# Fourier position steps: sums and differences of mirrored blocks written once, the first gate product reading them at exchanged places

## The chip, the cores and the metric

The kernel runs on one core of one Trainium2 chip. The metric is the device time of one execution in microseconds (us). Three executions took 1563.1, 1563.9 and 1565.81 us; the median is 1563.9 us.

## What is computed

The reference is a two-layer encoder trunk on two sequences, 2048 and 512 positions of 1024 channels, in fp32. Layer 0 is windowed attention. Layer 1, where the change lies, mixes by a Fourier transform in four groups of 256 channels:

```
h = rmsnorm(x, g)
hg = h.reshape(b, s, 4, 256)
f = fftn(hg, axes=(1, 3), norm="ortho").real.reshape(b, s, d)
x = x + (f * silu(h @ w_gate)) @ w_out
```

A final rmsnorm follows. The input is real, so the transform over a group's channels has a mirrored half: with A and B the two products of the position transform with the cosine and the sine columns, the real part at channel c is A - B or A + B, at the mirrored channel the other of the two; and the row of positions that mirrors a row has the two signs exchanged.

## The kernel before

**The order of the work.** First the attention runs, chunk by chunk. Then a Fourier phase (`fourier_phase`) runs through pairs of 128-position tiles: norm, transposes, channel transform (`z_odd_even`) and gate projection (`gates`). The results are combined over tiles by radix steps. From about 1296 us on come the *position steps*: each takes one residue k1 of the positions, multiplies it by cosine and sine tables (tile ABp in PSUM), multiplies by the gate and transposes the result (tile tw); `finish` then multiplies it with the output weights (tile fo) and adds the residual x. The steps run in the order s1, s0, s2 (the short sequence), p0 and p8, p4, p2, p6, and then p1, p7, p3, p5.

**Two blocks in a step.** p0, p8, s0 and s2 write one block of 128 output rows. The eight other steps write two: the row k1 and its mirror 16 - k1 (or 4 - k1). They take both from the same products A and B. The mirror's rows come out turned around, which the later transposes undo.

**What `position` (lines 1672 to 1714) does.** It works in two halves (`hf`) of two groups each. For each half it splits the operands (`halves_of`, line 1664, tile gp: a high part cast by the scalar engine and a low part subtracted by the vector engine), and three matmuls for each operand use them: high by high, high by low, low by high. Then, in each group of 256 columns, the columns 0 to 128 hold A (line 1701, copied by the scalar engine into the first block's tile up_0) and the sums and differences of A and B go as follows:

- up_1, columns 0 and 128: A, four elements copied by the scalar engine (line 1704)
- up_1, columns 1 to 127: A + B (line 1705); columns 129 to 255: A - B (line 1706)
- up_0, columns 129 to 255: A + B (line 1707); columns 1 to 127: A - B, in place (line 1708)

So a step with two blocks has four vector instructions of 128 x 254 elements per half, and one with a single block two (1707 and 1708). At the end the vector engine multiplies each tile of 1024 columns by its gate tile s2p (line 1711; 1713 for step s1, which hands the products to a list that runs later, after line 1473). The mirror's gate rows come by a gather on GpSimd's queue (line 1648), the other's by a load on SP's queue (line 1645).

**What sets the order.** Between s1 and p6 a scheduler orders each engine's instructions by priorities and by its own estimate of when operands are there, so that an edit of `position` moves the neighbours. From step p1 on, much of the vector engine's order is tied by hand (`seq`, `after`, `chain`). PSUM tiles, SBUF tiles of the pools "L", "R", "hT" and "x", and the queues of SP and GpSimd are taken in program order.

Of the kernel before, what the change touches and what calls it, by code (L numbers as in the profile page):

```python
# [14 lines left out]
ALU = mybir.AluOpType  # L15
# [5 lines left out]
P = 128  # L21
# [34 lines left out]
def encoder(  # L56
# [3 lines left out]
    PE, ACT, DVE, POOL, SP = nc.tensor, nc.scalar, nc.vector, nc.gpsimd, nc.sync  # L60
# [35 lines left out]
    def bank(name):  # L96
        if turning:
            return two_banks(name)[:, 0]
        return banks[-1].tile([P, 512], F32, tag="bank", name=name)
# [3 lines left out]
    def two_banks(name):  # L103
        return turning[0].tile([P, 2, 512], F32, tag="two", name=name)
# [29 lines left out]
    def matmul3(out, a, b, start, stop, more=False, behind=None):  # L134

        for i, j in ((0, 0), (0, 1), (1, 0)):
            ins = pe(PE.matmul(out, a[i], b[j], start=start and i + j == 0, stop=stop and i == 1, skip_group_check=more))  # L137
            after(ins, behind)
        return ins
# [53 lines left out]
    def after(ins, anchor):  # L193

        if anchor is not None:
            tc.add_manual_dep(ins.ins, anchor.ins.name, ISSUE, reason="issue order")
# [1022 lines left out]
    def fourier_phase(tail):  # L1219
        with ExitStack() as es:  # L1220
# [14 lines left out]
            def zt(name):  # L1235
                return right([P, D], F32, name)
# [167 lines left out]
            last_z, last_c, last_mix = [None], [None], [None] * 3  # L1404
# [246 lines left out]
            def position_loads(name, tab, tiles):  # L1651
                return [gated(name, r, xtile) for r in tiles], table(name, tab, left)

            def halves_of(name, gr, gs, hf, after_one=None):

                out = []
                for i, g in enumerate((gr, gs)):
                    if i and after_one:
                        after_one()
                    if g is not None:  # L1660
                        t = main.tile([P, 2, 512], F32R, align_bytes=LINE, tag="hT", bufs=8, name=f"g{name}_{hf}_{i}")
                        gv = g[hf] if isinstance(g, list) else g[:, hf * 512 : hf * 512 + 512]
                        ACT.copy(t[:, 0], gv)
                        low = DVE.tensor_tensor(t[:, 1], gv, f32(t[:, 0]), ALU.subtract)
                        if chain.get("steps"):
                            seq("dve", low)
                        out.append(t)
                return out

            last_b, last_read, gated_by = [None], [None], []  # L1670

            def position(name, tab, gr, gs, tiles, loads=None, parts=None, between=None, later=None):

                s2s, tb = loads or position_loads(name, tab, tiles)
                cs, sn, ns = [(tb[:, 2 * i], tb[:, 2 * i + 1]) for i in range(3)]
                bp = None if turning else bank(f"B{name}")
                us = [zt(f"u{name}_{i}") for i in range(len(tiles))]
                for hf in range(2):
                    if hf and between:
                        between()  # L1680
                    ts = parts[hf] if parts and parts[hf] else halves_of(name, gr, gs, hf)

                    def acc(out, tabs, c0, n):
                        for i, (w, t) in enumerate(zip(tabs, ts)):
                            v = [
                                t[:, part].rearrange("p (g c) -> p g c", g=2)[:, :, c0 : c0 + n]
                                for part in range(2)
                            ]
                            end = matmul3(out, w, v, i == 0, i == len(ts) - 1)
                        return end  # L1690

                    if turning:
                        ab = two_banks(f"AB{name}_{hf}")
                        a, b = ab[:, 0, :260], ab[:, 1, :256]
                    else:
                        a, b = bank(f"A{name}_{hf}")[:, :260], bp[:, hf * 256 : hf * 256 + 256]
                    a, b = (t.rearrange("p (g c) -> p g c", g=2) for t in (a, b))
                    chain["A"] = acc(a, (cs, ns), 0, 130)
                    chain["B"] = acc(b, (sn, cs), P, P)
                    uv = [u.rearrange("p (g c) -> p g c", g=4)[:, 2 * hf : 2 * hf + 2] for u in us]  # L1700
                    ACT.copy(uv[0][:, :, 0 : P + 1], a[:, :, 0 : P + 1])
                    re, im = uv[0][:, :, 1:P], b[:, :, 1:P]
                    for v in uv[1:]:
                        ACT.copy(v[:, :, 0 : P + 1 : P], a[:, :, 0 : P + 1 : P])
                        DVE.tensor_tensor(v[:, :, 1:P], re, im, ALU.add)
                        DVE.tensor_tensor(v[:, :, P + 1 : 256], re, im, ALU.subtract)
                    DVE.tensor_tensor(uv[0][:, :, P + 1 : 256], re, im, ALU.add)
                    last_b[0] = DVE.tensor_tensor(re, re, im, ALU.subtract)
                for u, s2 in zip(us, s2s):
                    if later is None:  # L1710
                        gated_by.append(DVE.tensor_tensor(u, u, s2, ALU.mult))
                    else:
                        later.append(lambda u=u, s2=s2: after(DVE.tensor_tensor(u, u, s2, ALU.mult), last_c[0]))
                return list(zip(us, tiles))

            def out_rows(r):
# [222 lines left out]
            def step(*positions):  # L1939
                new = [t for p in positions for t in position(*p)]  # L1940
                if pend:
                    end = finish(*pend.pop(0))
                if turning:
                    chain["turns"] = end
                    new = turned(new)
                else:
                    new = [(split_T(u, f"u{r[0]}", r[2] is not None), r) for u, r in new]
                for f in pend:
                    finish(*f)
                pend[:] = new  # L1950
# [48 lines left out]
            def sums_behind():  # L1999
# [10 lines left out]
                1: [lambda: f_load(1), lambda: early.append(sample(0, (0,), (left,), (xtile,), left, True))],  # L2010
                2: [lambda: f_load(2), lambda: early.append(sample(2, (1,), (left,), (xtile,), left, True))],
                3: [lambda: first.extend(position(*one, later=products)), lambda: f_load(3)],
                4: [lambda: [f() for f in products], lambda: f_load(4)],
                5: [lambda: turn_first(0), sums_behind],
                6: [lambda: turn_first(1)],
            })
            new = position(*early[0])
            f_split(4)
            new += position(*early[1])
# [12 lines left out]
            for i, l in enumerate((w0, w2)):  # L2032
                for a in range(3):
                    t = zt(f"ev{a}_{i}")
# [33 lines left out]
            for a in range(4):  # L2068
                for i, l in enumerate((pc, qs)):
# [3 lines left out]
                    t = zt(f"od{a}_{i}")  # L2073
# [205 lines left out]
```

## Time and profile before

| | |
|---|---|
| median of three executions | 1563.9 us |
| the profiled execution | 1564.1 us, its span 1562.3 us |
| tensor engine (PE) busy | 1545.1 us |
| vector engine (DVE) busy | 1148.0 us |
| scalar engine (ACT) busy | 889.3 us |
| GpSimd (POOL) busy | 454.5 us |
| mean granted clock of PE | 0.999 |

The span runs from the first to the last instruction; the time of an execution contains a little more. Times in the trace count from the span's start. A row of a timeline gives the start, the duration, the engine, the line of the code, the operation, the written tile, the tiles that are read, the shape and count; in brackets stands how long the engine sat idle before it and what ended that. PEld is the weight load of the tensor engine, which overlaps its matmuls. SPq and POOLq are the queues from which transfers are issued.

### The profile page before, as it was taken

To read this page: it belongs to the slowest core of one execution; us is meant where nothing else is said; L and a number is where in the kernel's file an instruction comes from. 1 tells how busy PE (TensorE), PEld (TensorE's weight loads), DVE (VectorE), ACT (ScalarE), POOL (GpSimd) and SP (SyncE) were. 2 spreads that over 40 slices of the span, in tenths; PEclk is the share of its full clock that TensorE was granted. 3 is DMA by queue.
4 is the path that set the end of the run, shared out by engine and by line. 5 is a ranking of instruction groups with operands and counts; after the bars stand their busy time and mean duration, and the time that the engine had idled before them with its cause. 6 is when DMAs were issued, how large, how long until landed. Compare 5 with 4: busy or idle time off the path is not lost.

```text
span 1562.3 us, 33420 instructions
## 1 busy us (share of the span) xinstructions
PE 1545.1 (99%) x12958; PEld 1355.5 (87%) x12958; DVE 1148.0 (73%) x2503; ACT 889.3 (57%) x1956; POOL 454.5 (29%) x616
## 2 busy tenths in 40 slices
PE   9999999999999999999999999999999999999998
PEld 7899888999898888988888899988888888888886
DVE  5888655777537776367764577768989888989896
ACT  6788534787237784257861477736656564333353
POOL 2565652421414313314214242223122211101100
PEclk9999999999999999999999999999999999999999
DMA  9677687685856765866639666665575669556852
GB/s 330 230 274 240 224 336 271 217 291 167 314 198 223 241 232 195 311 212 201 257 132 363 232 204 228 247 249 199 206 242 188 222 233 400 197 202 255 298 189 94
DMA packets 100730, 372.70 MB, mean 239 GB/s; under 512 B 11235, under 2 KB 22251, under 8 KB 83420
## 3 DMA queue, kind: packets, MB, share of 16 engines
q1 hardware_dynamic: 82716, 297.38, 55.3%
q0 software_dynamic: 16688, 70.04, 11.4%
q10 hardware_dynamic: 1168, 3.15, 0.6%
q8 instruction: 102, 1.67, 0.4%
q14 instruction: 56, 0.46, 0.1%
HBM read 280.06 MB, written 90.47 MB: 237 GB/s over the span
## 4 chain that ended last, share of the span: by engine, by line
PE 89%; DVE 6%; DMA 2%; ACT 1%; issue 1%; POOL 0%; POOLq 0%; ACTq 0%; DVEq 0%; SPq 0%
PE pj L527 27%; PE av L753 7%; PE W L137 6%; PE pj L137 6%; PE tp L137 5%; PE av L137 5%; PE spt L653 5%; PE spt L137 4%; PE tp L712 4%; PE Wo L137 3%; PE Z L137 3%; PE fo L137 3%; PE z L1392 2%; PE Zo L137 2%; PE X L137 1%; PE ABp L137 1%
## 5 line engine op out<-in xcount | busy, mean ns | idle before, releaser
L527 PE MATMUL pj<-h,wg 64*128 64x512 f32 x1920 | 438.9, 389 | 0.0
L527 PE MATMUL pj<-h,wq 64*128 64x512 f32 x1560 | 379.2, 389 | 1.2 <-DVE qab L571 1.2
L527 PEld LDWEIGHTS pj<-h,wg 64*128 64x128 f32 x1920 | 330.6, 184 | 23.1
L527 PEld LDWEIGHTS pj<-h,wq 64*128 64x128 f32 x1560 | 284.5, 184 | 22.0 <-DVE qab L571 2.7
L672 DVE CUSTOM_DVE_ANT_0 S<-spt,b 128x385 f32<-128x385 f32 (+1 forms) x320 | 165.1, 525 | 92.3 <-PE spt L653 88.3
L680 ACT ACTIVATE S<-S 128x385 f32<-128x385 f32 (+1 forms) x320 | 189.1, 592 | 63.2 <-DVE S L672 41.6
L725 ACT CAST pts<-tp 128x768 fp32r<-128x768 f32 (+1 forms) x160 | 121.2, 758 | 95.4 <-PE av L753 60.0
L729 DVE TENSOR_TENSOR pts<-tp,pts 128x768 fp32r<-128x768 f32 (+1 forms) x160 | 144.1, 901 | 13.5 <-ACT pts L725 12.8
L753 PE MATMUL av<-pts,v 64*128 64x256 f32 x1680 | 143.5, 287 | 3.0 <-DVE pts L729 3.0
L753 PEld LDWEIGHTS av<-pts,v 64*128 64x128 f32 x1680 | 127.2, 186 | 7.3 <-DVE pts L729 3.8
L798 POOL TENSOR_TENSOR uT<-o,uT 128x256 fp32r<-128x256 f32 x75 | 56.7, 756 | 244.1 <-ACT uT L794 243.9
L653 PE MATMUL spt<-kwin,qab 64*128 64x384 f32 (+1 forms) x960 | 121.0, 338 | 0.9 <-DVE S L672 0.7
L137 PE MATMUL fo<-wo,tTu 128*128 128x512 f32 x480 | 115.1, 392 | 0.0
L137 PEld LDWEIGHTS fo<-wo,tTu 128*128 128x128 f32 x480 | 88.4, 188 | 17.3
L712 PEld LDWEIGHTS tp<-ident,S 64*128 64x128 f32 x1792 | 93.2, 137 | 10.2 <-DVE pts L729 3.1
L712 PE MATMUL tp<-ident,S 64*128 64x64 f32 x1792 | 97.9, 224 | 0.1
L789 POOL TENSOR_TENSOR o<-o,s 128x256 f32<-128x256 f32 x75 | 55.7, 742 | 120.7 <-DVE o L783 95.3
L695 DVE TENSOR_SCALAR S<-S 128x384 f32<-128x384 f32 (+1 forms) x192 | 89.6, 495 | 0.1
L653 PEld LDWEIGHTS spt<-kwin,qab 64*128 64x128 f32 x960 | 84.8, 187 | 3.8 <-issue 1.8
L282 DVE SCALAR_TENSOR_TENSOR h<-xk,g0s,h 128x512 fp32r<-128x512 f32 x40 | 44.6, 1124 | 49.7 <-ACT h L281 49.5
L527 PE MATMUL pj<-wo,uT 64*128 64x512 f32 x360 | 74.8, 390 | 0.0
L281 ACT ACTIVATE h<-xk,g0s 128x512 fp32r<-128x512 f32 x40 | 28.8, 724 | 73.7 <-POOL xk L277 73.2
(380 smaller groups left out, 3414.1 us busy)
## 6 DMA issues: line engine op xcount, KB each, us to landing
wo<-wsd SPq DMA_DIRECT2D x32, 1024.0 KB, 6.0
wq<-wsd SPq DMA_DIRECT2D x31, 1024.0 KB, 6.0
wg<-wsd SPq DMA_DIRECT2D x31, 1024.0 KB, 5.8
x<-x1d SPq DMA_DIRECT2D x40, 512.0 KB, 4.0
b<-b21d SPq DMA_DIRECT2D x40, 512.0 KB, 5.8
b<-rowd SPq DMA_DIRECT2D x40, 384.0 KB, 4.1
xs<-in_x_dram SPq DMA_DIRECT2D x23, 512.0 KB, 6.1
s2d<-gt POOLq DMA_DIRECT2D x40, 256.0 KB, 4.4
```

Of the source, the lines that this page charges most:

```text
L137: ins = pe(PE.matmul(out, a[i], b[j], start=start and i + j == 0, stop=stop and i == 1, skip_group_check=more))
L527: out.last[h] = pe(PE.matmul(out.ps, a[i], b[j], **out.flags()))
L653: pe(PE.matmul(spt[j][:, 2 + k0 * P : 2 + k1 * P], res["q"][rows, qp, b * P : (b + 1) * P], kwin[g][rows, kp, b * P + k0 * P : b * P + k1 ...
L672: seq(DVE, DVE.tensor_tensor_reduce(out=s[:, e0:e1], in0=ps[:, 1 + e0 : 1 + e1], in1=st["bias"][:, j, 386 - e1 : 386 - e0][:, ::-1], scale ...
L680: last_exp[0] = seq(ACT, ACT.activation(s[:, e0:e1], s[:, e0:e1], AF.Exp, bias=s[:, 386:387], scale=-1.0, accum_out=s[:, 387:388]))
L695: seq(DVE, DVE.tensor_scalar(s[:, ks], s[:, ks], den, None, ALU.mult))
L712: pe(PE.transpose(ps[h][:, kb, j, :], s[rows, j, 1 + kb * P : 1 + (kb + 1) * P], ident[rows, rows]))
L725: seq(ACT, ACT.copy(hi, ps))
L729: seq(DVE, DVE.tensor_tensor(lo, ps, f32(hi), ALU.subtract))
L753: last[i][h] = pe(PE.matmul(av[:, i, :256], v[rows], pt[rows], start=not swap and n == 0, stop=swap and n == len(todo[h]) - 1, skip_group_ ...
L789: eng.tensor_tensor(o, o, s, ALU.mult)
L798: low = eng.tensor_tensor(lo, o, f32(hi), ALU.subtract)
```

## The change

The sums and differences are formed once for each half, in the tile of the last block (`us[-1]`): the mirror's in a step with two blocks, the only one otherwise. The scalar engine copies A's 129 columns there. Columns 129 to 255 get the difference and columns 1 to 127 the sum, in a step with two blocks; in a step with one block the signs are as before. The first block's tile up_0 is no longer filled. Its gate product reads up_1 with the two 128-column parts of each group exchanged, and writes up_0. Columns 0 and 128 of each group must not be exchanged, so a second product of 128 x 8 elements writes them again. The mirror's gate product is in place and comes last.

```diff
-                    ACT.copy(uv[0][:, :, 0 : P + 1], a[:, :, 0 : P + 1])
-                    re, im = uv[0][:, :, 1:P], b[:, :, 1:P]
-                    for v in uv[1:]:
-                        ACT.copy(v[:, :, 0 : P + 1 : P], a[:, :, 0 : P + 1 : P])
-                        DVE.tensor_tensor(v[:, :, 1:P], re, im, ALU.add)
-                        DVE.tensor_tensor(v[:, :, P + 1 : 256], re, im, ALU.subtract)
-                    DVE.tensor_tensor(uv[0][:, :, P + 1 : 256], re, im, ALU.add)
-                    last_b[0] = DVE.tensor_tensor(re, re, im, ALU.subtract)
+                    v = uv[-1]
+                    ACT.copy(v[:, :, 0 : P + 1], a[:, :, 0 : P + 1])
+                    re, im = v[:, :, 1:P], b[:, :, 1:P]
+                    two = (ALU.add, ALU.subtract)[:: -1 if len(us) > 1 else 1]
+                    DVE.tensor_tensor(v[:, :, P + 1 : 256], re, im, two[0])
+                    last_b[0] = DVE.tensor_tensor(re, re, im, two[1])
+
+                def by_gates(u, s2):
+                    if u is us[-1]:
+                        return DVE.tensor_tensor(u, u, s2, ALU.mult)
+
+                    to, src, s = (t.rearrange("p (g h c) -> p g h c", g=4, h=2) for t in (u, us[1], s2))
+                    DVE.tensor_tensor(to, src[:, :, ::-1], s, ALU.mult)
+                    return DVE.tensor_tensor(to[:, :, :, 0], src[:, :, :, 0], s[:, :, :, 0], ALU.mult)
+
...
-                        gated_by.append(DVE.tensor_tensor(u, u, s2, ALU.mult))
+                        gated_by.append(by_gates(u, s2))
...
-                        later.append(lambda u=u, s2=s2: after(DVE.tensor_tensor(u, u, s2, ALU.mult), last_c[0]))
+                        later.append(lambda u=u, s2=s2: after(by_gates(u, s2), last_c[0]))
```

In the changed kernel the new lines are 1702 (copy), 1705 and 1706 (sums and differences), 1710 (gate product in place), 1713 (the exchanged product) and 1714 (its eight columns); what followed line 1714 before has a number higher by 7.

The change also moves other instructions. The first place is the tensor engine ahead of step p0: its first two ABp matmuls, which need the high parts of gp, among the fo matmuls of the short sequence's last product (fo_0 with the tile tTu_0 that is written last). Before:

```order
L137 MATMUL fo_1_17856<-wo_17747,tTu_1_17649 128x512 x3
L137 MATMUL fo_0_17981<-wo_17431,tTu_0_17733 128x512 x3
L137 MATMUL fo_0_17981<-wo_17433,tTu_0_17733 128x512 x2
L137 MATMUL ABp_0_17923<-gp_0_0_17920,tbp_17917 128x260
L137 MATMUL fo_0_17981<-wo_17433,tTu_0_17733 128x512
L137 MATMUL fo_0_17981<-wo_17455,tTu_0_17733 128x512
L137 MATMUL ABp_1_17936<-gp_1_0_17933,tbp_17917 128x260
```

And in the changed kernel:

```order
L137 MATMUL fo_1_17851<-wo_17742,tTu_1_17644 128x512 x3
L137 MATMUL fo_0_17976<-wo_17431,tTu_0_17728 128x512
L137 MATMUL ABp_0_17918<-gp_0_0_17915,tbp_17912 128x260
L137 MATMUL fo_0_17976<-wo_17431,tTu_0_17728 128x512
L137 MATMUL ABp_1_17931<-gp_1_0_17928,tbp_17912 128x260
L137 MATMUL fo_0_17976<-wo_17431,tTu_0_17728 128x512
```

The first ABp matmul stood behind five fo matmuls of that product and now stands behind one.

The second place is the vector engine between step p4 and the operands of step p2. x_0 is a residual tile, invf its norm, tc and od are tiles of the radix combination of odd residues, tm is what the scalar engine makes for them from loaded tiles od. Before:

```order
L1758 TENSOR_TENSOR x_0_18218<-x_0_18218,fo_1_18246 128x512
L2082 SCALAR_TENSOR_TENSOR tc_18402<-od_0_18392,tm_18400 128x1024
L130 TENSOR_SCALAR invf_18275<-ssf_18272 128x1
L1276 TENSOR_TENSOR tTu_0_18314<-tw_18280,tTu_0_18314 128x512
L1728 SCALAR_TENSOR_TENSOR x_0_18218<-x_0_18218,invf_18275,gfb 128x1024
L1276 TENSOR_TENSOR tTu_0_18317<-tw_18297,tTu_0_18317 128x512
L1276 TENSOR_TENSOR tTu_1_18320<-tw_18280,tTu_1_18320 128x512
L2084 SCALAR_TENSOR_TENSOR od_1_18394<-od_1_18394,tm_18400 128x1024
```

And in the changed kernel:

```order
L1765 TENSOR_TENSOR x_0_18208<-x_0_18208,fo_1_18236 128x512
L130 TENSOR_SCALAR invf_18265<-ssf_18262 128x1
L1735 SCALAR_TENSOR_TENSOR x_0_18208<-x_0_18208,invf_18265,gfb 128x1024
L1276 TENSOR_TENSOR tTu_0_18304<-tw_18270,tTu_0_18304 128x512
L1276 TENSOR_TENSOR tTu_0_18307<-tw_18287,tTu_0_18307 128x512
L2089 SCALAR_TENSOR_TENSOR tc_18392<-od_0_18382,tm_18390 128x1024
L1276 TENSOR_TENSOR tTu_1_18310<-tw_18270,tTu_1_18310 128x512
L1276 TENSOR_TENSOR tTu_1_18313<-tw_18287,tTu_1_18313 128x512
```

The first tc, which stood between the residual sum and the norm, now stands behind the norm's scaling and two low parts (tTu). On SP's queue the load of x_8 now stands ahead of five of the six od loads where it stood ahead of three, and the first od load stands behind one more output; further down, the low part gp_0_1<-g2s follows gp_0_0<-g2r directly, where z and x_8's second sum stood between, and gp_1_1<-g2s stands behind x_8's scaling and two of the sums of p2. On GpSimd's queue the gather of p2's gate rows (s2p_14) moves behind one more norm.

The third place is the tensor engine at step p6: the first matmuls that need the low parts of its operands. Before:

```order
L137 MATMUL fo_0_18760<-wo_17558,tTu_1_18580 128x512 x3
L137 MATMUL fo_0_18760<-wo_17560,tTu_1_18580 128x512
L137 MATMUL ABp_0_18702<-gp_0_0_18671,tbp_18698 128x260 x2
L137 MATMUL ABp_0_18702<-gp_0_1_18674,tbp_18698 128x260
L137 MATMUL fo_0_18760<-wo_17560,tTu_1_18580 128x512
L137 MATMUL ABp_0_18702<-gp_0_1_18674,tbp_18698 128x260 x2
```

And in the changed kernel:

```order
L137 MATMUL fo_0_18740<-wo_17552,tTu_1_18565 128x512 x3
L137 MATMUL fo_0_18740<-wo_17554,tTu_1_18565 128x512 x3
L137 MATMUL fo_1_18766<-wo_17676,tTu_0_18559 128x512 x3
L137 MATMUL ABp_0_18687<-gp_0_0_18656,tbp_18683 128x260 x2
L137 MATMUL ABp_0_18687<-gp_0_1_18659,tbp_18683 128x260
L137 MATMUL fo_1_18766<-wo_17679,tTu_0_18559 128x512
```

They stood behind 22 of the fo_0 matmuls and now stand behind all 24 and three of fo_1.

## The prediction

> **What bounds the kernel now.** First the page: its span, the tensor engine's row and the granted clock.
>
> ```profile
> span 1562.3 us, 33420 instructions
> PE 1545.1 (99%) x12958; PEld 1355.5 (87%) x12958; DVE 1148.0 (73%) x2503; ACT 889.3 (57%) x1956; POOL 454.5 (29%) x616
> PEclk9999999999999999999999999999999999999999
> ```
>
> The tensor engine is busy in 1545.1 of 1562.3 us, and its clock is never held back. A busy matmul row need not mean that the engine is at its pace, so next comes the chain of work that ended last, which gives starts: twelve matmuls of 512 columns, and twelve of 260 or 256.
>
> ```profile
> 1541.70 2.72 PE Wo L137 x12
> 1452.35 1.44 PE ABp L137 x12
> ```
>
> That is 0.227 us and 0.12 us for one. The step code runs only in the tail, after about 1296 us, so I then asked what the tensor engine waited for there (total us, times, longest).
>
> ```profile
> PE ABp L137 <- DVE gp L1664: 1.2, 2, 0.8
> PE ABp L137 <- ACT gp L1663: 0.7, 1, 0.7
> PE W L137 <- DVE c L1473: 0.3, 1, 0.3
> ```
>
> All that a faster vector or scalar engine could give back is 1.2 + 0.7 + 0.3 = 2.2 us, or 0.14% of the run. The timeline of the tensor engine says where the ABp waits lie (start, duration, what, idle before it):
>
> ```profile
> 1323.71 12.51 PE L137 MATMUL fo<-wo,tTu 128*128 128x512 f32 x54
> 1336.93 0.39 PE L137 MATMUL ABp<-gp,tbp 128*128 128x260 f32 x1 [0.71 <-ACT gp L1663]
> 1388.33 0.78 PE L137 MATMUL ABp<-gp,tbp 128*128 128x260 f32 x5
> 1390.67 2.55 PE L137 MATMUL ABp<-gp,tbp 128*128 128x260 f32 x19 [0.40 <-DVE gp L1664]
> 1421.31 0.63 PE L137 MATMUL ABp<-gp,tbp 128*128 128x260 f32 x3 [0.79 <-DVE gp L1664]
> 1530.73 1.21 PE L115 MATMUL tw<-ident,up 64*128 64x64 f32 x32
> ```
>
> Place A is the first position step (p0, 0.71), place B step p2 (0.40), place C step p6 (0.79). The last row, the turning transposes of step p5, starts with no wait, like those of the steps ahead of it. The busy times by stretch show why B and C wait (columns: stretch, its length, PE, PEld, DVE, ACT, POOL busy, PEclk, DMA share, GB/s).
>
> ```profile
> 1360.00:1380.00 20.00, 20.00 (x127) 16.90 (x126) 13.23 (x23) 6.66 (x14) 2.11 (x3) 1.00 0.75 279
> 1380.00:1400.00 20.00, 19.60 (x98) 16.40 (x97) 19.27 (x29) 9.38 (x17) 0.86 (x2) 1.00 0.35 119
> 1400.00:1420.00 20.00, 20.00 (x117) 16.42 (x116) 19.44 (x25) 6.73 (x12) 2.84 (x3) 1.00 0.30 100
> 1420.00:1440.00 20.00, 19.21 (x121) 15.86 (x120) 18.81 (x29) 4.84 (x11) 3.33 (x3) 1.00 0.89 334
> ```
>
> From 1380 to 1440 the vector engine is full too. There a vector instruction less can matter; elsewhere it is cover that nobody needs.
>
> **What goes and what comes.** The instructions by line (xcount: shortest/median/longest ns), and one step's run on the vector engine:
>
> ```profile
> L1704 ACT COPY up<-ABp x14: 165/172/176, 1364.6 to 1524.3; 128x4 f32<-128x4 f32 x14
> L1705 DVE TENSOR_TENSOR up<-up,ABp x14: 412/415/417, 1366.5 to 1525.1; 128x254 f32<-128x254 f32 x14
> L1711 DVE TENSOR_TENSOR up<-up,s2p x16: 1218/1221/1226, 1342.8 to 1528.1; 128x1024 f32<-128x1024 f32 x16
> L312 DVE COPY g0s<-av x1: 167/167/167, 3.7 to 3.7; 128x8 f32<-128x8 f32 x1
> ```
>
> ```profile
> 1366.51 0.41 DVE L1705 TENSOR_TENSOR up<-up,ABp 128x254 f32<-128x254 f32 x1
> 1366.84 0.41 DVE L1706 TENSOR_TENSOR up<-up,ABp 128x254 f32<-128x254 f32 x1
> 1369.95 0.41 DVE L1708 TENSOR_TENSOR up<-up,ABp 128x254 f32<-128x254 f32 x1
> 1370.39 1.23 DVE L1711 TENSOR_TENSOR up<-up,s2p 128x1024 f32<-128x1024 f32 x1
> 1376.27 0.69 DVE L1758 TENSOR_TENSOR x<-x,fo 128x512 f32<-128x512 f32 x1 [4.05 <-PE fo L137]
> ```
>
> Eight two-block steps (s1, p4, p2, p6, p1, p7, p3, p5) lose two sums or differences and one small copy per half: 32 vector instructions and 16 scalar ones. Starts lie 0.33 apart (1366.51, 1366.84), so a step loses 4 x 0.33 = 1.32 us of the vector queue, not 4 x 0.415 = 1.66. The Trainium skill, VectorE: DVE Perf Modes, section "The DRAIN you can't avoid", has the next operation start only when the pipe is empty. By that rule the step would lose the 1.66; the spacing of the rows decides against it.
>
> Each step gains one 128x8 product. The trace has none; the nearest row is the 128x8 copy, 0.17 us, the lower end is nothing and the upper end that of a 128x254 row, 0.41. I take 0.17. So a step is 1.15 us shorter on the vector engine. The first gate product now reads the mirrored row with its blocks exchanged and writes another tile. It still handles 1024 elements of the same type; no row shows blocks read in reverse order from such a tile, so its cost lies between nothing and, if it ran at half pace, 1.2 us more; I take nothing, by the row of the same size. The scalar copies (0.17 each) lie on an engine that is 57% busy, behind the operands that the matmuls wait for: nothing.
>
> In the four late steps (p1, p7, p3, p5) this gain is worth nothing: the transposes start without a wait already. Step p4's saving is lost in the 4.05 us in which the vector engine then waits for fo (row 1376.27). In s1 the first gate product now stands ahead of c<-c,W, on which W waits for 0.3; it takes up 1.2 us where 4 x 0.33 went away: 0.
>
> **Place A.** The order shows the first ABp one fo matmul into its product where it stood five matmuls in: the tensor engine reaches it 4 x 0.227 = 0.9 us sooner. What it needs is made here:
>
> ```profile
> 1335.01 1.22 DVE L1502 TENSOR_TENSOR r<-e,f 128x1024 f32<-128x1024 f32 x1
> 1336.26 1.14 ACT L1663 CAST gp<-r 128x512 fp32r<-128x512 f32 x2 [8.55 <-DVE r L1502]
> ```
>
> The cast sat idle 8.55 us for r, and nothing ahead of r moves in the vector queue or among the loads. So gp is ready no sooner, and the wait grows from 0.71 to 1.6: +0.9. The bounds are 0 (if r were 0.9 earlier) and +0.9. All behind it shifts alike, the vector engine too, since it waits for fo in row 1376.27.
>
> **Place B.** Step p2's operands, and the work around them on three engines:
>
> ```profile
> 1376.26 1.06 ACT L2080 ACTIVATE tm<-od 128x1024 f32<-128x1024 f32 x1 [10.46 <-DMA od<-odd]
> 1377.35 1.23 DVE L2082 SCALAR_TENSOR_TENSOR tc<-od,tm 128x1024 f32<-128x1024 f32 x1 [0.40 <-ACT tm L2080]
> 1378.50 0.15 DVE L130 TENSOR_SCALAR invf<-ssf 128x1 f32<-128x1 f32 x1
> 1379.47 1.28 DVE L1728 SCALAR_TENSOR_TENSOR x<-x,invf,gfb 128x1024 f32<-128x1024 f32 x1
> 1387.59 0.69 DVE L1664 TENSOR_TENSOR gp<-g2r,gp 128x512 fp32r<-128x512 f32 x1
> 1389.92 0.69 DVE L1664 TENSOR_TENSOR gp<-g2s,gp 128x512 fp32r<-128x512 f32 x1
> 1369.97 1.51 SPq L2074 DMA_DIRECT2D od<-odd  x3
> ```
>
> Now tc filled the time in which the norm is under way (1377.35 to 1378.50, 1.15 us). In the new order it stands behind the scaling and two low parts (tTu), and that gap stays empty. The list up to gp<-g2r is otherwise the same, so its end moves from 1388.28 to about 1389.4. The tensor engine asks for it two short matmuls after 1388.33, at 1388.6: a wait of 0.8. In return gp<-g2s stands directly behind, ready 0.6 later, at 1390.0, and is asked for 3 x 0.12 + 0.227 after 1389.4, at 1390.0: the old wait of 0.40 goes. Net +0.4. The second half's last operand now stands behind a scaling and two sums; its product is asked for 17 fo matmuls after the first half's, where it was hardly any before. I find both near 1395.3 and put 0.2 on it. Bounds for B: -0.4 (both waits gone) and +2.0 (0.8 - 0.4 + 0.2, doubled, and 0.8 for a late second half).
>
> SP issues five od loads behind the load of x_8 where it issued three (row 1369.97) and two sooner. At the stretch's 279 GB/s a load of 512 KB takes 1.9 us, so the one that tm waits for may land 3.8 later, at 1380.1, and tm end at 1381.2; tc's new turn is at about 1379.2 + 1.2 + 2 x 0.6 = 1381.6. It is just covered.
>
> **Place C.** Rows for p6's operand, the last gate of p5, and on GpSimd the gather that is moved past one more norm:
>
> ```profile
> 1420.57 1.29 DVE L1664 TENSOR_TENSOR gp<-ev,gp 128x512 fp32r<-128x512 f32 x2
> 1528.12 1.22 DVE L1711 TENSOR_TENSOR up<-up,s2p 128x1024 f32<-128x1024 f32 x1
> 1371.90 1.00 POOL L1648 DMA_INDIRECT s2p<-s2d,mir  x1 [6.63 <-DVE up L1711]
> 1396.12 1.22 DVE L1711 TENSOR_TENSOR up<-up,s2p 128x1024 f32<-128x1024 f32 x1
> ```
>
> The vector queue comes to p6 with 1.15 more behind it from B and 1.15 less from p2's sums: level. It may lose up to 1.1 in waiting for p2's second half, which the tensor engine now does some 2.9 later. So gp is ready between 1421.2 and 1422.3. The order has the matmul that needs it five fo matmuls later, 1.13; with B's 0.6 it is asked for at 1421.31 - 0.79 + 1.13 + 0.6 = 1422.2. The wait nearly goes: -0.8, with bounds -0.8 and +0.5. p5's last gate ended at 1529.34, 1.4 ahead of its transposes, and ends sooner now. The gather waits for x_0's norm, near 1379.5, and is used at 1396: hidden.
>
> **Sum.** +0.9 + 0.4 + 0.2 - 0.8 = +0.7 us. The profiled execution took 1564.1 us (span 1562.3 and 1.8 around it), 0.2 above the median of 1563.9. So 1564.8 by its count, **1564.6** by the median's. The ends: -0.4 - 0.8 - 0.3 = -1.5, 1562.4; and 0.9 + 2.0 + 0.5 = +3.4, 1567.3. A measurement of this kernel can tell about 0.2%, 3.1 us, from no change.
>
> **Rivals.** (1) *All waits go*: the shorter vector queue is ahead everywhere, 2.2 us less, 1561.7. The full vector rows speak for it; the earlier ABp at A speaks against. Chance 0.08. (2) *The vector engine paces the tail*, matmul spacing being slack: 32 x 0.33 - 8 x 0.17 = 9.2 us less, 1554.7. Against it: twelve matmuls in 2.72 us where nothing waits, as everywhere. Chance 0.05. The Trainium skill, TensorE: Matmul & The Clock Gate, section "Back-to-back issue gap", gives about 131 ns per 512-column matmul sustained in a real kernel, by which the tensor engine would have such slack; the 227 ns here say that it has not. (3) *Late od loads*: from a landing past 1380.4 on, each us is one us at B, since the vector queue there has no slack; at 1383.4 it is +3.0 beside the +0.7, 1567.6, slower. Against it: 3.8 late is an upper end. Chance 0.10. (4) *The exchanged reading runs at half pace*: p2's share of 1.2 undoes its saving, C keeps its wait, and B's transposes stay covered: 1.2 more, 1565.8. Chance 0.05. My forecast has 0.72.
>
> Faster by over 0.2% is rival 2 and a hundredth of rest: 0.06. Slower is rival 3: 0.10. Within 0.2%: 0.84. Leaving out rival 2, the end of 1 and the far part of 3, the range is 1562.2 to 1567.0.
>
> **What would show it.** In the new trace: 24 vector instructions fewer in all (32 less 8), a 128x8 row near 0.17, the exchanged product at 1.22; ABp waits of about 1.6 at A (ACT gp), 0.8 at B, none at C; no wait of the transposes tw. It is wrong if ABp's total wait leaves the 1 to 4 us, if the product is over 1.3 us, or if the tensor engine's busy time changes at all.

## The result and the profile after

The changed kernel's median is 1566.59 us (22 executions, 1565.95 to 1571.41) beside 1564.9 us for the kernel before on the same chip (22 executions, 1563.1 to 1568.17). The ratio is 1.0013, with a 95% interval from 1.0007 to 1.0019: 1.7 us slower by the medians, where +0.7 was forecast, and inside the 0.2% that were counted as no change. It is 2.0 us above the forecast of 1564.6 us; 1.0 of that is the kernel before, whose median was 1563.9 us in three executions and is 1564.9 in 22.

The page of the changed kernel, profiled once: span and busy times.

```profile
span 1564.2 us, 33377 instructions
PE 1546.2 (99%) x12958; PEld 1355.7 (87%) x12958; DVE 1139.8 (73%) x2479; ACT 887.9 (57%) x1940; POOL 457.0 (29%) x616
```

The vector engine has 24 instructions and 8.2 us less to do, and the span is 1.9 us longer. The new lines cost what the forecast said (shortest, median, longest ns):

```profile
L1713 DVE TENSOR_TENSOR up<-up,s2p x7: 1210/1224/1226, 1368.0 to 1527.2; 128x1024 f32<-128x1024 f32 x7
L1714 DVE TENSOR_TENSOR up<-up,s2p x7: 167/171/180, 1369.3 to 1529.2; 128x8 f32<-128x8 f32 x7
```

So the time is not in the instructions. What the tensor engine waited for in the tail (total us, times, longest):

```profile
PE ABp L137 <- DVE gp L1664: 1.8, 2, 1.0
PE Wo L137 <- DVE x L1839: 0.9, 1, 0.9
PE ABp L137 <- ACT gp L1663: 0.6, 1, 0.6
```

The middle row is new. The tensor engine's timeline at the three places of the forecast, and at a fourth, D, in step p1:

```profile
1335.94 0.39 PE L137 MATMUL ABp<-gp,tbp 128*128 128x260 f32 x1 [0.56 <-ACT gp L1663]
1389.76 0.65 PE L137 MATMUL ABp<-gp,tbp 128*128 128x260 f32 x3 [0.98 <-DVE gp L1664]
1423.26 0.63 PE L137 MATMUL ABp<-gp,tbp 128*128 128x260 f32 x3 [0.79 <-DVE gp L1664]
1451.14 3.02 PE L137 MATMUL Wo<-fT,S 128*128 128x512 f32 x12 [0.87 <-DVE x L1839]
```

The start of each step's first transpose (tile tw) cuts the tail into stretches that can be compared between profiles. From step p0's to step p4's it is 26.06 us in all fourteen profiles of this study. The others, in us:

| profile | p4 to p2 (place B) | p2 to p6 (C) | p6 to p1 (D) | p1 to p5 | p0 to p5 |
|---|---|---|---|---|---|
| before | 26.76 | 32.65 | 25.02 | 70.14 | 180.63 |
| changed | 27.52 | 32.66 | 26.03 | 70.18 | 182.45 |
| difference | +0.76 | +0.01 | +1.01 | +0.04 | +1.82 |

From p1's transposes to p5's, a stretch with the new code of three of the four late steps, it is the same to 0.04 us. The loss of this pair behind p0 is B and D.

**Place A.** Step p0's transposes start at nearly the same time in this pair, but that is the sum of two differences. The cast that p0's first matmuls wait for started at 1336.26 before. Then came, before,

```profile
1350.10 1.21 PE L115 MATMUL tw<-ident,up 64*128 64x64 f32 x32
```

and in the changed kernel

```profile
1335.27 1.14 ACT L1663 CAST gp<-r 128x512 fp32r<-128x512 f32 x2 [8.41 <-DVE r L1502]
1350.15 1.21 PE L115 MATMUL tw<-ident,up 64*128 64x64 f32 x32
```

The cast comes 0.99 us sooner, and from the cast to the transposes it is 14.88 us for 13.84.

**Place B.** The vector engine there, in the changed kernel:

```profile
1378.27 0.15 DVE L130 TENSOR_SCALAR invf<-ssf 128x1 f32<-128x1 f32 x1 [1.27 <-ACT jkf L1283]
1379.16 1.28 DVE L1735 SCALAR_TENSOR_TENSOR x<-x,invf,gfb 128x1024 f32<-128x1024 f32 x1 [0.73 <-POOL invf L131]
1381.56 1.21 DVE L2089 SCALAR_TENSOR_TENSOR tc<-od,tm 128x1024 f32<-128x1024 f32 x1
1389.03 0.68 DVE L1664 TENSOR_TENSOR gp<-g2r,gp 128x512 fp32r<-128x512 f32 x1
1395.00 0.69 DVE L1664 TENSOR_TENSOR gp<-g2s,gp 128x512 fp32r<-128x512 f32 x1
1397.42 0.42 DVE L1705 TENSOR_TENSOR up<-up,ABp 128x254 f32<-128x254 f32 x1 [1.74 <-ACT up L1702]
```

tc, which had filled the time of the norm, comes at 1381.56, and 1.27 + 0.73 us stay empty; gp<-g2r comes at 1389.03 for 1387.59. Then the last gp<-g2s comes at 1395.00, where the kernel before had finished both by 1391.8; the second half's product is made later, and the vector engine stands 1.74 us for its copy. Its busy time by stretch, before and then after:

```profile
1376.00:1401.00 25.00, 24.60 (x146) 20.53 (x145) 23.39 (x34) 13.12 (x22) 2.42 (x3) 1.00 0.47 173
```

```profile
1376.00:1401.00 25.00, 24.02 (x143) 19.93 (x142) 20.44 (x29) 12.76 (x20) 3.15 (x3) 1.00 0.50 178
```

It stands 4.56 us for 1.61: the 1.15 us that the change saves in step p2 and 1.8 us more are lost in waiting. gp<-ev of step p6 starts at 1422.52 for 1420.57.

**Place D.** That lateness goes on through two queues. The scalar engine's queue issues the writes god when the vector engine has made them, SP's queue the loads fT, which wait there for god, and behind them and one output write the load of x_6. Before, and then after:

```profile
1423.03 0.33 ACTq L2114 DMA_DIRECT2D god<-g3r  x1
1423.66 3.22 SPq L1928 DMA_DIRECT2D fT<-fT1d  x4
1428.37 7.68 SPq L1928 DMA_DIRECT2D fT<-fT2d  x4
1438.28 0.86 SPq L1739 DMA_DIRECT2D x<-x1d  x2
1448.59 0.69 DVE L1832 TENSOR_TENSOR x<-x,Wo 128x512 f32<-128x512 f32 x1 [3.33 <-DMA x<-x1d]
```

```profile
1424.98 0.37 ACTq L2121 DMA_DIRECT2D god<-g3r  x1
1425.10 6.34 SPq L1935 DMA_DIRECT2D fT<-fT1d  x4
1431.55 8.15 SPq L1935 DMA_DIRECT2D fT<-fT2d  x4
1441.27 0.91 SPq L1746 DMA_DIRECT2D x<-x1d  x2
1450.40 0.69 DVE L1839 TENSOR_TENSOR x<-x,Wo 128x512 f32<-128x512 f32 x1 [1.41 <-DMA x<-x1d]
```

What SP's queue waited for in the changed kernel between 1400 and 1460 has the landing of that write (before, the same row had 1.2):

```profile
SPq L1935 <- DMA god<-g3r: 3.7, 1, 3.7
```

The load goes out 2.99 us later, its sum comes 1.81 later, and the accumulation tile Wo, which that sum must have read before it is written again, holds up the tensor engine for 0.87 us. The kernel before stood at the brink of this: the vector engine waited there as well (3.33 us), but in time for the tensor engine.

### The profile page after: what moved, and what is told of

The parts are those of the page before. It is cut to its first block, busy times and chain, and to the rows that moved or that the text cites. A ratio compares the mean times of both kernels' runs of the same rounds, so it can differ in the third digit from the quotient of the medians.

```text
span 1564.2 us, 33377 instructions
## 1 busy us (share of the span) xinstructions
PE 1546.2 (99%) x12958; PEld 1355.7 (87%) x12958; DVE 1139.8 (73%) x2479; ACT 887.9 (57%) x1940; POOL 457.0 (29%) x616
## 4 chain that ended last, share of the span: by engine, by line
PE 86%; DVE 6%; DMA 4%; ACT 2%; issue 1%; POOL 0%; SPq 0%; POOLq 0%; ACTq 0%; DVEq 0%
PE pj L527 27%; PE av L753 7%; PE pj L137 5%; PE W L137 5%; PE tp L137 5%; PE av L137 5%; PE spt L653 5%; PE spt L137 4%; PE tp L712 3%; PE Wo L137 3%; PE fo L137 3%; PE Z L137 3%; PE z L1392 2%; PE Zo L137 2%; PE ABp L137 1%; PE X L137 1%
```

## The experiments

**Theory.** The tensor engine sets the end, so the instructions taken away and added are worth nothing by themselves; the loss is the new order between steps p4 and p6 (B) and what follows from the vector engine's lateness in p1 (D). **Rivals.** The new instructions cost; what lies ahead of p0 costs; the late steps gain or lose by the vector engine's time. Four of the fourteen profiles are 1.4 to 1.8 us longer in their first 170 us, in code that no kernel here changes, so the stretches of the table are the finer measure and the medians the check on the whole.

**e1, the change in the late steps alone.** In `position` the old block stands in an else branch of

```diff
+                    if chain.get("steps"):
+                        v = uv[-1]
...
+                    else:
+                        ACT.copy(uv[0][:, :, 0 : P + 1], a[:, :, 0 : P + 1])
...
-                    if u is us[-1]:
+                    if u is us[-1] or not (chain.get("steps")):
```

> The four late steps (p1, p7, p3, p5) have the new sums and the exchanged product, everything ahead of them has the old code, and the PE order is that of before. Theory (the moved order of the early tail costs the time, the instructions themselves cost and bring nothing): within 0.3 us of before, ratio 0.9998 to 1.0002, no wait of Wo for x in step p1. Rival (the new instructions themselves cost, above all the exchanged product or the product of 8 elements): four of the seven tail steps have them, so about half of the 1.9 us or more, ratio 1.0006. Rival (DVE time in the late steps is worth something): 4 x 1.15 us shorter, ratio 0.998 or less.

Measured: ratio 1.0001 (0.9992 to 1.0009); p4 to p2 27.04, p2 to p6 32.64, p6 to p1 25.04, p1 to p5 70.14 us; no wait of Wo. Sixteen vector instructions out, eight scalar ones out and four small products in change nothing, neither way. (p2's transposes start at 1402.95, as before; p0's came 0.25 us earlier in this profile, and that was spent in waiting for p2's operands.)

**e2, the change everywhere else.** The same with `not chain.get("steps")`.

> The complement: new code in s1, p4, p2 and p6, old code in the four late steps. Theory: the whole loss is there, both the 0.98 us wait of ABp for gp<-g2r in step p2 and the wait of Wo for x in step p1; 1.5 to 1.9 us over before, ratio 1.0010 to 1.0012. Rival (the instructions themselves cost): a half or less, ratio 1.0005.

Measured: ratio 1.0021 (1.0012 to 1.0030); 27.50, 32.65, 26.09 us: B +0.74, C 0, D +1.07, the whole loss. The median is 3.6 us over before, above the forecast of 1.5 to 1.9; the stretch from p0 to p5 explains 1.8 of that (more under e12).

**e3, one place of the order put back.** The first tc is tied ahead of x_0's scaling (`chain["x", 0]` is that scaling, kept in `norm`).

```diff
-                DVE.scalar_tensor_tensor(c_, pc[a], ca, tmp, ALU.mult, S)
+                ins = DVE.scalar_tensor_tensor(c_, pc[a], ca, tmp, ALU.mult, S)
+                if a == 1:
+                    after(chain["x", 0], ins)
```

> The changed kernel with one tie of order: DVE makes the first tc ahead of the scaling of x_0, as before the change. Theory: the wait of ABp for gp<-g2r falls from 0.98 to 0.4 or less, DVE is 1 to 2 us earlier through p6, the god writes with it, and the wait of Wo for x goes: within 0.5 us of before, ratio 0.9997 to 1.0003. Rival (the instructions cost, or the loads ahead of p0): 1.7 to 1.9 us over before stay, ratio 1.0011. Rival (half of it: the wait at p2 goes, the W wait has another cause and stays): ratio 1.0006.

Measured: ratio 1.0019 (1.0010 to 1.0027); 27.27, 32.68, 25.79 us: B +0.51, D +0.77. The waits of the tail behind p0:

```profile
PE ABp L137 <- DVE gp L1664: 1.2, 2, 0.8
PE Wo L137 <- DVE x L1840: 0.6, 1, 0.6
PE ABp L137 <- DVE invf L130: 0.2, 1, 0.2
```

The theory in this form falls: a third of B goes and a quarter of D, no more. gp<-g2r is back at 1387.39, but now the second half waits, whose gp<-g2s the vector engine makes behind x_8's scaling, at 1394.20.

**e4, D by itself.** The changed kernel with the loads of x_6 and x_10 on GpSimd's queue.

```diff
...
-            o.load()
+            o.load(POOL)
```

> The changed kernel with the two residual loads x_6 and x_10 issued on POOL's queue, not behind the eight fT loads on SP. Theory: they land some us earlier, the 0.87 us wait of Wo for x in step p1 goes and with it about 1.0 us: 0.7 to 0.9 us over before, ratio 1.0005, with the wait at p2 unchanged at 0.98. Rival (DVE, 1.9 us late, makes PE wait for the next operand instead): still 1.7 to 1.9 us over before, ratio 1.0012, with a wait on DVE elsewhere in step p1.

Measured: ratio 1.0015 (1.0006 to 1.0024); 27.52, 32.68, 24.83 us. The wait of Wo is gone, and the wait at p2 is the same:

```profile
PE ABp L137 <- DVE gp L1664: 1.8, 2, 1.0
PE ABp L137 <- ACT gp L1663: 0.7, 1, 0.7
1451.85 2.45 PE L137 MATMUL Wo<-fT,S 128*128 128x512 f32 x10
```

D is 1.2 us less (24.83 for 26.03), 0.2 below before. So D is the place of that load on SP's queue, and the vector engine's lateness makes no other wait in its stead. The median doesn't show it: it is 2.35 us over before, of which the stretch from p0 to p5 explains 0.6 (more under e12).

**e5, the order without the change.** The kernel before with the first tc tied behind x_0's scaling: its line becomes `after(DVE.scalar_tensor_tensor(...), chain["x", 0])`.

> The kernel before, with none of the new instructions, and one tie of order: DVE makes the first tc behind the scaling of x_0, as the changed kernel does. Measured from the first transpose into tru, near 1305 us, to the end, which leaves out the first 170 us whose length differs from one execution to the next by up to 2 us (250.2 us before, 252.2 us after). Theory: the order alone brings the loss, step p2's matmuls wait longer for gp<-g2r, DVE idles for the copies of p2, reaches p6 over 1 us late, and Wo waits for x in p1: 1.0 to 2.5 us more than 250.2. Rival (the new instructions cost): 250.2, within 0.3 us. The median 1.0 to 2.5 us over before, ratio 1.0006 to 1.0016.

```profile
PE ABp L137 <- ACT gp L1663: 1.2, 1, 1.2
PE Wo L137 <- DVE x L1833: 0.7, 1, 0.7
PE ABp L137 <- DVE gp L1664: 0.6, 2, 0.3
```

Measured: ratio 1.0001 (0.9991 to 1.0011); 26.94, 32.21, 25.78 us: B +0.18, C -0.44, D +0.76. From the first transpose into the tile tru, near 1305 us, to the last matmul it is 251.3 us for 250.2, of which 0.5 lies ahead of p0. So D comes with not one new instruction in the kernel. But B hardly does, and C gains: the order that follows from this tie is not that of the changed kernel on the tensor engine. One place of the order is not the whole of the change's order.

**e6, both places put back.** To e3's tie is added, in `halves_of`,

```diff
+                        if (name, hf, i) == ("p2", 1, 1):
+                            after(chain["x", 8], low)
```

which puts the last gp<-g2s ahead of x_8's scaling.

> The changed kernel with two ties of order: the first tc ahead of the scaling of x_0, and the low half of the last gp<-g2s of step p2 ahead of the scaling of x_8, both as before the change. Theory: step p2's second half no longer comes late, DVE no longer idles some 1.4 us for its copy, p6 comes 1 us earlier, the god writes and the load of x_6 with it, and the wait of Wo goes or falls under 0.2 us: from tru to the end 250.0 to 250.7 us. Rival (the two places are independent: the load of x_6 waits behind the fT loads for another reason): 251.0 to 251.4, as with one tie, with a Wo wait of 0.5 us or more.

Measured: ratio 1.0010 (1.0000 to 1.0019); 26.61, 32.95, 25.45 us: B -0.15, C +0.30, D +0.43. B is gone with all the new instructions in place. Why C is longer stays open. D is halved, not gone, with a wait of Wo of 0.4 us. (From tru to the end this profile is longer than both forecasts: 3.4 us ahead of p0, of which more below.)

**e7 and e8, the vector engine's cover in the late steps.** The kernel before with four and with eight more sums a step (2 and 4 in each half), whose results are overwritten:

```diff
+                    for i in range(2 * ("steps" in chain)):
+                        DVE.tensor_tensor(uv[0][:, :, P + 1 : 256], re, im, ALU.add)
```

> The kernel before with four more sums of 128x254 in each of the four late steps, their results overwritten: 4 x 0.33 = 1.32 us of DVE time more a step, as the change takes 1.15 away. Theory (DVE time in the late steps is covered by PE, with about 1.4 us to spare in front of the transposes): 0 to 0.3 us over before, from tru to the end 250.2 to 250.5. Rival (DVE paces the late steps): 4 x 1.32 = 5.3 us over before, ratio 1.0034.

> The same with eight more sums, 2.64 us of DVE time more a step. Theory: the 1.4 us of cover is used up and the rest is paid in each of four steps: 4 x (2.64 - 1.4) = 5 us over before, from tru to the end about 255, ratio 1.0032, with a wait of the transposes for DVE in each late step. Rival (DVE paces them already): 10.6 us, ratio 1.0067. Rival (more cover than that, since the order can shift): under 2 us.

The transposes of the four late steps in e7, and then in e8:

```profile
1461.85 1.21 PE L115 MATMUL tw<-ident,up 64*128 64x64 f32 x32 [0.66 <-DVE up L1713]
1485.57 1.22 PE L115 MATMUL tw<-ident,up 64*128 64x64 f32 x32 [0.25 <-DVE up L1713]
1509.35 1.21 PE L115 MATMUL tw<-ident,up 64*128 64x64 f32 x32 [0.34 <-DVE up L1713]
1533.06 1.21 PE L115 MATMUL tw<-ident,up 64*128 64x64 f32 x32 [0.27 <-DVE up L1713]
```

```profile
1464.03 1.20 PE L115 MATMUL tw<-ident,up 64*128 64x64 f32 x32 [1.98 <-DVE up L1713]
1489.06 1.20 PE L115 MATMUL tw<-ident,up 64*128 64x64 f32 x32 [1.59 <-DVE up L1713]
1515.34 1.21 PE L115 MATMUL tw<-ident,up 64*128 64x64 f32 x32 [1.26 <-DVE up L1713]
1540.36 1.21 PE L115 MATMUL tw<-ident,up 64*128 64x64 f32 x32 [1.57 <-DVE up L1713]
```

Ratios 1.0013 (1.0002 to 1.0025) and 1.0056 (1.0038 to 1.0074). The cover is there and smaller than I took it: 1.32 - 0.27 = 1.05 us of p5's step, not 1.4, and 1.32 - 0.66 = 0.66 in p1, where the vector engine has also stood 3.24 us for x_6. So the 0 to 0.3 us forecast for e7 became 1.76 from p0 to p5 (182.39 us), and the 5 for e8 8.1 (188.75). Past the cover each us is paid. From e7 to e8 the wait grows by 1.32, 1.34 and 1.30 us in p1, p7 and p5: four sums cost 4 x 0.33, their spacing, and not 4 x 0.415, their length. In p3 it grows by 0.92 only, which stays unexplained. e8's loss goes beyond the 6.4 us of its waits by the clock (below).

**e9, the changed kernel once more.**

> The changed kernel as it is, profiled once more: how far the places repeat. From the first transposes of p0's result to the end: 206.9 us in its first profile, 205.1 before. Theory (the loss is in the order of the instructions, and so the same each time): 206.6 to 207.1, again a wait of 0.9 to 1.0 us for gp<-g2r and one of 0.8 to 1.0 us of Wo for x, while the wait of ABp for gp ahead of p0 comes out otherwise (0.3 to 2.5 us in the profiles so far, also between kernels whose code is the same there). Rival (the two waits are chance, as the one ahead of p0 is): 205 to 206.5. Median ratio to before 1.0013, as in its first timing.

```profile
PE ABp L137 <- ACT gp L1663: 1.9, 1, 1.9
PE ABp L137 <- DVE gp L1664: 1.8, 2, 1.0
PE Wo L137 <- DVE x L1839: 0.8, 1, 0.8
```

Measured: median 1567.01 beside 1564.89, ratio 1.0016 (1.0007 to 1.0025); 27.51, 32.69, 25.92 us: B +0.75, C +0.04, D +0.90. B, C and D repeat to 0.1 us. The wait ahead of p0 does not: 1.9 us here and 0.56 above, in one and the same kernel.

**e10, e1 and e4 together:** the old code ahead of the late steps, the change in the late steps, the two loads on GpSimd's queue.

> The candidate that should be no worse than either kernel: new code in the four late steps alone, the order ahead of them that of before, and the loads of x_6 and x_10 on POOL's queue. Theory: as the late-only kernel, less what W still loses in p1 before the change, 0.2 to 0.3 us: from p0 to the end 204.8 to 205.1 us, ratio to before 0.9997 to 1.0000, too little for the median to tell. Rival (POOL's queue brings them late as well, or takes something from the gathers there): 205.4 or more.

Measured: ratio 0.9998 (0.9989 to 1.0007); 26.84, 32.64, 24.72, 70.15 us; p0 to p5 180.41 for 180.63. It is 0.2 us better in the stretches, which no median here can tell from no change.

**e11, e6 and e4 together:** the whole change, both ties, the two loads on GpSimd's queue.

> The changed kernel with both ties and the loads of x_6 and x_10 on POOL's queue, which should take away every part of the loss that was found behind p0. Theory: from p0 to the end 205.1 us, within 0.4 of before (p0 to p2 52.7 to 52.9, p2 to p6 32.6 to 32.9, p6 to p1 24.8 to 25.0), with no wait of Wo for x. Rival (something else in the changed kernel costs too): 205.8 or more. The median: ratio to before 1.0000 to 1.0005, apart from what the wait ahead of p0 adds by chance.

Measured: ratio 1.0007 (0.9998 to 1.0016); 26.62, 32.96, 24.72 us; p0 to p5 180.52: B -0.14, C +0.31, D -0.30, together 0.11 below before. No wait of Wo is left. With every new instruction in place the stretches are back where they were, and 0.11 us above those of e10, which has the same two loads on that queue: the loss of the changed kernel behind p0 was order, and with it the turn of one load on SP's queue.

**e12, the order ahead of p0.** As e1, with `name[0] == "s"` for the condition: the change in s1 alone, and the changed kernel's order ahead of p0.

> New code in the sample step s1 alone (its two tiles), old code from p4 on: the order ahead of p0 is that of the changed kernel, with the gate casts of the sums ahead of the scaling of x_2051 and the first four matmuls for gp earlier, the order behind it that of before. The medians of the seven kernels with the changed order ahead of p0 so far lie on average 1.1 us further over before than their stretch from p0 to the end explains, those of the kernels with the old order there 0.0 us. Theory A (the order ahead of p0 costs about 0.9 us in the mean over executions, as forecast for that place, and single profiles hide it in a wait of 0.3 to 2.5 us): median 0.7 to 1.5 us over before, ratio 1.0004 to 1.0010. Theory B (it costs nothing there): ratio 0.9997 to 1.0003. Both: from p0 to the end 205.0 to 205.4 us, as before. The interval of a timing is some 0.0009 either way, so that only a value near an end tells.

Measured: ratio 1.0002 (0.9993 to 1.0011), median 1565.01 beside 1565.33; p0 to p5 180.46. Place A in its profile:

```profile
1336.03 0.39 PE L137 MATMUL ABp<-gp,tbp 128*128 128x260 f32 x1 [0.28 <-ACT gp L1663]
```

The median lies where theory B has it, but its interval takes in theory A as well, and the profile shows a price of the order: from the cast to p0's transposes it is 14.88 us, as in the changed kernel. The total hides it, since the cast starts 30.09 us after the first tru here and 31.33 after it before. The other profiles agree. From the cast to the transposes it is 13.83 to 13.87 us in the six with the old order ahead of p0 (before, e1, e5, e7, e8, e10) and 14.88 or 14.89 in six of the eight with the new order; in the other two, e6 and e9, it is 16.23, with half clock behind the wait (last section). So the order costs 1.03 us from the time that gp is there. When gp is there differs by more than that between the profiles of either order: the cast starts 30.5 to 32.5 us after the first tru with the old, 30.1 to 32.3 with the new.

The medians lean to theory A. Less what the stretch from p0 to p5 explains, those of e2, e3, e4, e6 and e11, all with the new order ahead of p0, are 0.9 to 1.8 us over before; the changed kernel's two timings and e12 are at -0.1, +0.4 and -0.15; the mean of the eight is 0.9. With the old order e1, e5, e7 and e10 are at -0.4 to +0.3; e8, with its waits near 2 us, is at 1.4. One timing is uncertain by about 1.4 us, so what place A costs in the mean stays open.

## Why the prediction was right, and where not

- **That the tensor engine paces the tail, and late steps gain nothing**: right. e1 is its direct test: 25.04 us from p6 to p1 for 25.02, and 70.14 from p1 to p5 for 70.14. The cover at p5 was 1.05 us where I read 1.4 from the end of a product to the start of the transposes; not all of that gap can be used.
- **The prices** (0.33 a sum, 0.17 the small product, the exchanged reading like the plain one): right; 0.171 and 1.224 us in the new profile, 0.33 by e7 and e8. The Trainium skill, VectorE: DVE Perf Modes, section "The DRAIN you can't avoid", from which the prediction takes 1.66, also has a next operation that is not held start earlier. The 0.33 agrees with that.
- **Place A, +0.9**: right in the step, and hidden in the pair that was compared. The fo matmuls ahead start 0.84 us sooner (1322.87 for 1323.71), and from the cast on the new order takes 1.03 us more, in every profile that has it. The step that failed is "gp is ready no sooner". The ev loads that r is made from are issued at 1310.80 for 1311.36 here and the cast follows at 1335.27 for 1336.26, which leaves +0.05. In e9, the same kernel, the cast starts 31.73 us after the first tru, for 30.38 in the first profile, and the wait is 1.94. So the +0.05 is the chance of this pair and no refutation of the price; whether the new order also brings gp sooner in the mean (30.8 us after the first tru for 31.5), eight profiles against six don't show. I had a gp 0.9 earlier as the lower bound.
- **Place B, +0.6**: measured +0.76, right in kind and near in size. gp<-g2r came at 1389.03 with a wait of 0.98 (forecast 0.8). That the wait only moves to the second half when the tc is put back (e3), and goes with both (e6), I had not seen.
- **Place C, -0.8**: measured +0.01. The step that failed is the vector queue coming "level" to p6, at most 1.1 us late. It came 1.95 late (1422.52 for 1420.57), as the empty stretches of 1.27 + 0.73 and 1.74 us took more than the saving of 1.15; so the matmul that was asked for later still waited 0.79.
- **Place D, +1.0**: not foreseen. I followed the vector engine's lateness to the next operand and no further; its results are also written out, a queue waits for those writes, and a load stands behind. That e4 takes D away with one queue, and e5 makes it without the change, shows it.
- **The sum**: +0.05 + 0.76 + 0.01 + 1.01 = +1.8 us, for +0.7 forecast. Two errors of about 0.8 with opposite signs at A and C cancelled, and D is what was missing. 1566.59 us is within the range of 1562.2 to 1567.0 because that had been drawn over the bounds of A, B and C; that it holds is in part luck, since the largest loss was in none of its terms.
- **The rivals**: the waits did not all go (1), the vector engine does not pace the tail (2), the exchanged reading is at full pace (4). In place of late od loads (3) a late residual load cost the time.

## What to carry to other kernels

Work taken from an engine that another one covers was worth nothing here, sixteen instructions of it; how much cover there is can be measured by adding work until the time moves. When a scheduler orders the rest, an edit's price can be in what it moves: put single places back by a tie, and do the edit in one part of the program alone, to split instructions from order. Follow a lateness through every queue that it feeds, the writes and the loads behind them too; and compare stretches between fixed instructions of two profiles where whole executions differ by chance, and cut the stretch where the chance comes in, as at the cast ahead of p0: one pair of totals hid 1.03 us there.

## What was not expected of the hardware

**Behind a wait of the tensor engine its clock can fall to half.** In e9, after the wait of 1.94 us that ends at 1339.60 (columns as in the windows above; the third from the end is the granted clock):

```profile
1338.00:1340.00 2.00, 0.40 (x2) 0.30 (x2) 1.97 (x2) 1.07 (x2) 0.00 (x0) 1.00 0.04 16
1340.00:1342.00 2.00, 2.00 (x8) 1.55 (x8) 2.00 (x5) 1.83 (x4) 0.00 (x0) 0.77 0.58 154
1342.00:1344.00 2.00, 2.00 (x10) 1.90 (x9) 1.55 (x4) 0.81 (x3) 0.87 (x1) 0.50 0.27 109
1344.00:1346.00 2.00, 2.00 (x10) 1.73 (x10) 2.00 (x5) 0.38 (x1) 0.58 (x1) 0.88 0.10 41
```

2 x (0.23 + 0.50 + 0.12) = 1.7 us are lost, as by 3.4 us at half clock. e6 has the same behind a wait of 2.5 us, e8 behind those of 1.59 and 1.57 us (0.79 over the 8 us from 1489, 0.86 over the 12 us from 1540: 1.7 us each), but not behind those of 1.9 and 1.98 us. e2 has it far ahead of the change, behind a wait of 1.39 us (av is a product of the attention, pts its operand):

```profile
89.46 0.62 PE L753 MATMUL av<-pts,v 64*128 64x256 f32 x5 [1.39 <-DVE pts L729]
92.00:94.00 2.00, 2.00 (x15) 1.63 (x13) 1.40 (x6) 1.98 (x6) 0.74 (x1) 0.50 1.06 385
```

All fourteen profiles have that wait of 1.39 us, and the clock falls in e2 alone. Of the 29 waits of 1.35 to 1.41 us in these profiles one was followed by half clock, of the six of 1.57 to 2.5 us four; while matmuls run it falls nowhere else. So such a wait costs about twice its length or more in some executions and its length in others. The Trainium skill, TensorE: Matmul & The Clock Gate, section "Part 1: The HAM clock gate (the "warmup" mystery)", has the clock fall to half after an idle window of about 3.4 us that runs free of the program. The half and the 3.4 us agree with these rows; that the idle time must be that long does not, since 1.39 us were enough here.

**The first 170 us differ between executions.** Counted matmul by matmul, e2, e4, e9 and e10 are 1.4 to 1.8 us behind the profile of before at 170 us, the other nine of these kernels within 0.35 us, with the same instructions. In e2 it is the half clock above; e4, e9 and e10 have lost theirs by the matmul that starts at 23 us before, at full clock, and why is open. The wait ahead of p0 for gp differs too, from none in e10 to 2.5 us. Together they are about the size of what the change cost.
